# A two-layer recurrent trunk on one core: the adaLN modulation computed on VectorE, GpSimd and ScalarE instead of TensorE

## The chip, the core and the metric

One core of one Trainium2 chip runs the kernel. The metric is the device time of one execution in microseconds (us). TensorE (PE) multiplies matrices, VectorE (DVE), ScalarE (ACT) and GpSimd (POOL) do elementwise work, SyncE (SP) issues most DMAs. Each engine takes its own instructions in the order of the program; engines wait for one another by semaphores.

## What is computed

A decoder trunk of two layers over 1024 tokens of width 1024, all in float32. Layer 0 mixes tokens by RWKV-7, layer 1 by a gated DeltaNet; each is followed by a dense SwiGLU layer. Before each sublayer the tokens are scaled and shifted, and after it gated, by a modulation that depends on one vector `c` alone:

```python
cond = jax.nn.silu(c)                                   # c is (1, 1024)
for i in range(2):
    mod = (cond @ ada_w[i] + ada_b[i])[:, None, :]      # 1024 x 6144, every layer
    sh1, sc1, ga1, sh2, sc2, ga2 = jnp.split(mod, 6, axis=-1)
    u = x * (1 + sc1) + sh1
    y = mixer_i(u)                                      # RWKV-7, then gated DeltaNet
    x = layer_norm(ALPHA * x + (1 + ga1) * y)
    u = x * (1 + sc2) + sh2
    gate, up = jnp.split(u @ ffn_w_in[i], 2, axis=-1)
    x = layer_norm(ALPHA * x + (1 + ga2) * ((silu(gate) * up) @ ffn_w_out[i]))
```

RWKV-7 first interpolates each token with the one before it, in six mixtures (`lerp`): `k`, `v` and `r` are products of three of them with 1024x1024 weights, and three small ones (decay, rate, gate) of the others with 1024x64 or 1024x128 weights. The modulation is a matrix-vector product: 2 x 1024 x 6144 weights, 50 MB, each used once.

## The kernel before

**Tiles.** Features lie on the partitions in KT = 8 blocks of 128, tokens on the free axis, in two halves of 512. A large product is taken in float32 accuracy by three matmuls per block of 128x128: weight and operand are each split into a rounded part and a remainder (`split`, L220: ACT casts the rounded part, POOL or DVE subtracts it), and `mm3` (L261 to L266) adds hi x hi, hi x lo and lo x hi. One product of 128 rows with a half is 8 x 3 = 24 matmuls of 512 columns. `weight` (L241) loads 512 KB (tile `wr`, two buffers) and splits it into `wh` and `wl` (three buffers each); at the first use it also saves `wl` to DRAM, and at the second it loads it back, so that only ACT's cast (L252) is left.

**Stages**, with their places in the profiled execution. A (0 to 230 us): layer 0's modulation and the first half's k, v and r products. B (to 684): RWKV units of the first half, woven with the second half's products. C (684 to 1335): RWKV units of the second half, woven with dense work of the first (output projection, norm, SwiGLU layer) and with layer 1's modulation. Then a "turn" (1335 to some 1680): the second half's output projection, norms, and first products of the DeltaNet, among them those with the weights `w_g`. Then DeltaNet units woven with the second half's dense layer, a second turn, and the same for the other half.

`weave`, `interleave` and `drive` set the order in which pieces of two or three generators are recorded, by costs given by hand. A scheduler then places the instructions on each engine, so that the order on an engine is not simply that of the code.

**Modulation before** (`ada`, L279). The column of silu(c) lies in `condr`, 128 x 8 x 32, with zeros in 31 of 32 columns (`cond_columns`, L274). A matmul takes it as the stationary operand and 128 rows by 512 or 256 columns of the weights as the moving one (L296), in plain float32, with four blocks of k side by side in the array (`tile_position`). The four partial rows are copied by ACT (L301), transposed by PE (L305) so that the result lies along partitions, summed by DVE (L307), and the bias is added. Layer 0 takes 12 pieces of 512 columns, layer 1 takes 24 of 256. Loads come from SP, two of 512 KB a piece in layer 1, four in layer 0.

**Start before** (`proj_rwkv`, L355). Pieces 0 and 2 of layer 0 (shift and scale of the feature blocks 0 to 3) come first; then four tiles of x are modulated on DVE (`make_x`, L366) and mixed (`lerp`, L380); the first half of k of the first NH = 5 products follows with half weights (`half_weight`, `half_product`); pieces 1 and 3 are run between these, and the second half of k comes when they are done. In the loop behind it, each step loads and splits its own weight and small weight, and multiplies. `rest()` (in `main`) puts the other eight pieces between the products.

**Where layer 1's modulation lay**: 24 pieces in stage C alone, with PSUM banks of their own kind and one buffer for loaded weights.

Of the kernel before, what the change touches and what calls it, by code (L numbers as in the profile page):

```python
# [27 lines left out]
        ("lng", 32), ("lnb", 32), ("adab", 96), ("conv", 96), ("ng", 1), ("c", 8), ("alog", 8), ("dtb", 8)]  # L28
# [29 lines left out]
def body(ctx, tc, A):  # L58
# [55 lines left out]
    def mm_ps():  # L114
        return bank("mm")
# [9 lines left out]

    def ad_ps():
        return bank("ad")
# [140 lines left out]
    cond = tl(cp, [P, KT], F32, "cond")  # L268
    sigmoid(cond[:, :], V("c", 0, 8))
    tt(dve, cond[:, :], cond[:, :], V("c", 0, 8), MUL)  # L270
# [3 lines left out]
    def cond_columns(pl):  # L274
        condr = pools["condr"] = tl(pl, [P, KT, 32], F32, "condr")
        dve.memset(condr[:, :, :], 0.0)
        dve.tensor_copy(out=condr[:, :, 0], in_=cond[:, :])

    def ada(ap, l, j, n=512, bufs=4, ps=None, bk=mm_ps):  # L279

        condr = pools["condr"]
        w = 1024 // n
        pst = None
        for q in range(KT // w):
            raw = tl(ap, [P, w, n], F32, "ada", bufs)
            (act if q % 2 == 0 and not ps and ADQ and j > 3 else sync).dma_start(
                out=raw[:, :, :],
                in_=A["ada_w"][l, P * w * q:P * w * (q + 1), n * j:n * j + n].rearrange("(k p) c -> p k c", p=P))
            if ps:
                yield 1.0  # L290
            if pst is None:
                pst = (ps or bk)()
            for k in range(w):
                kt = w * q + k
                g = kt % 4
                pe.matmul(pst[32 * g:32 * g + 32, 0:n], condr[:, kt, :], raw[:, k, :], start=(kt < 4), stop=(kt >= 4),  # L296
                          tile_position=(0, 32 * g))
        if ps:
            yield 0.4
        row = e_tile()  # L300
        act.copy(out=row[:, 0:n], in_=pst[:, 0:n])  # L301
        pc = (ps or bk)()
        m = n // P
        for i in range(m):
            pe.transpose(pc[:, P * i:P * i + P], row[:, P * i:P * i + P], C("ident"))  # L305
        o = mod[l][:, m * j:m * j + m]
# [7 lines left out]
        elif f % 3 == 2:  # L314
            ts2(dve, o1, o, 1.0, (0.5 if f == 5 else 1.0) / ALPHA, ADD, MUL)
# [39 lines left out]
    def proj_rwkv():  # L355
# [72 lines left out]
        for k in range(4):  # L428
            load_x(0, k)
# [1196 lines left out]
```

## Time and profile before

| | us |
|---|---|
| three runs | 3346.52, 3362.83, 3360.3 |
| their median | 3360.3 |
| the profiled execution | 3353.55 |
| its span (first to last instruction) | 3351.8 |
| mean granted TensorE clock in it | 0.976 |

A row of a timeline reads: start in us, duration in us, engine, line, operation, out<-in by the program's names, shape, count of instructions put together, and in brackets the idle time of the engine just before and what ended it. A row of a group has the count, then busy us and mean ns, then idle time before. Chain of waits: PE's three matmul lines hold 10% each of the chain that ended last, no other line more than 1%. The busy tenths of PE, POOL and DMA in 40 equal slices of 84 us:

```profile
PE   7989999998999999898999999999999999999997
...
POOL 3563232355454443455521000230244543520001
...
DMA  7773334253445444645754555566654546565553
```

The first slice holds the start, in which PE is at seven tenths. The zeros of POOL are the stages of the DeltaNet units.

### The profile page before, as it was taken

What the parts mean: (1) busy time and instruction counts of PE and PEld (TensorE: products, weight loads), DVE (VectorE), ACT (ScalarE), POOL (GpSimd) and SP (SyncE); (2) the same over time, 40 slices, a digit from 0 to 9 for tenths busy, and PEclk for the clock granted to TensorE, in tenths of its full rate; (3) what the DMA queues carried; (4) which work ended last, traced back from release to release, by engine and by line L of the source; (5) the groups of instructions that cost most, each with busy time, mean ns of one, the idle gap of its engine ahead of it and who ended that gap; (6) DMA issues with size and microseconds to landing.
All of it is one profiled execution on the core that took longest, in us unless ns stands there. A gap on an engine that the chain in (4) does not pass through costs nothing. (4 is left out here: it accounts for less than half of the span.)

```text
span 3351.8 us, 52009 instructions
## 1 busy us (share of the span) xinstructions
PE 3189.0 (95%) x19152; PEld 2459.8 (73%) x19152; DVE 2073.8 (62%) x4549; ACT 1409.7 (42%) x2735; POOL 1133.4 (34%) x1354
## 2 busy tenths in 40 slices
PE   7989999998999999898999999999999999999997
PEld 4667777776777767676877778777777777878886
DVE  5557888888666666586476555575477653563235
ACT  4665777644333332355432322365432322332222
POOL 3563232355454443455521000230244543520001
PEclk8999999998999999999999999999999999999998
DMA  7773334253445444645754555566654546565553
GB/s 262 271 244 103 113 105 132 96 183 113 163 168 170 162 154 148 215 170 189 248 192 165 185 172 174 195 200 226 219 173 144 175 167 216 176 213 181 197 183 130
DMA packets 240527, 594.13 MB, mean 177 GB/s; under 512 B 24720, under 2 KB 80656, under 8 KB 240272
## 3 DMA queue, kind: packets, MB, share of 16 engines
q1 hardware_dynamic: 240128, 590.74, 51.9%
q8 instruction: 150, 2.46, 0.3%
q14 instruction: 105, 0.86, 0.1%
q10 hardware_dynamic: 144, 0.07, 0.0%
HBM read 440.04 MB, written 150.67 MB: 176 GB/s over the span
## 5 line engine op out<-in xcount | busy, mean ns | idle before, releaser
L264 PE MATMUL mm<-s,wh 128*128 128x512 f32 x2608 | 1076.9, 413 | 12.2 <-DVE e L215 5.4
L265 PE MATMUL mm<-s,wh 128*128 128x512 f32 x2608 | 1051.6, 403 | 12.3 <-POOL s L212 7.9
L266 PE MATMUL mm<-s,wl 128*128 128x512 f32 x2608 | 1046.0, 401 | 0.0
L212 POOL TENSOR_TENSOR wl<-wr,wh 128x256 fp32r<-128x256 f32 (+1 forms) x828 | 653.8, 821 | 845.3 <-ACT wh L222 784.1
L264 PEld LDWEIGHTS mm<-s,wh 128*128 128x128 f32 x2608 | 495.0, 190 | 131.3 <-issue 25.1
L265 PEld LDWEIGHTS mm<-s,wh 128*128 128x128 f32 x2608 | 495.7, 190 | 105.4 <-POOL s L212 11.9
L266 PEld LDWEIGHTS mm<-s,wl 128*128 128x128 f32 x2608 | 495.4, 190 | 93.1 <-issue 0.4
L252 ACT CAST wh<-wr 128x1024 fp32r<-128x1024 f32 x199 | 206.8, 1049 | 496.0 <-PE mm L265 238.5
L222 ACT CAST wh<-wr 128x1024 fp32r<-128x1024 f32 (+1 forms) x254 | 228.7, 906 | 342.0 <-PE mm L265 181.2
L215 DVE SCALAR_TENSOR_TENSOR x<-mm,modp,x 128x512 f32<-128x512 f32 x272 | 202.0, 747 | 76.6 <-PE mm L266 74.7
L264 PE MATMUL mm<-ys,wh 128*128 128x512 f32 x544 | 219.3, 403 | 5.8 <-DVE x L215 5.8
L265 PE MATMUL mm<-ys,wh 128*128 128x512 f32 x544 | 217.5, 400 | 0.0
L266 PE MATMUL mm<-ys,wl 128*128 128x512 f32 x544 | 217.2, 399 | 0.0
L215 DVE SCALAR_TENSOR_TENSOR e<-e,vec,e 128x512 f32<-128x512 f32 x144 | 124.1, 865 | 97.2 <-ACT e L1306 94.6
L212 DVE TENSOR_TENSOR e<-mm,e 128x512 f32<-128x512 f32 x88 | 60.6, 689 | 167.3 <-PE mm L266 167.0
L215 DVE SCALAR_TENSOR_TENSOR e<-e,mm 128x512 f32<-128x512 f32 x88 | 60.2, 684 | 144.8 <-ACT e L679 144.5
L838 PEld LDWEIGHTS <-z 128*128 128x128 f16 x1600 | 84.0, 98 | 82.8 <-issue 47.7
L215 DVE SCALAR_TENSOR_TENSOR tx<-mm,modp,tx 128x512 f32<-128x512 f32 x112 | 83.1, 747 | 78.5 <-PE mm L266 78.2
L212 DVE TENSOR_TENSOR s<-e,s 128x512 fp32r<-128x512 f32 x106 | 85.8, 811 | 69.5 <-ACT s L222 69.2
L264 PEld LDWEIGHTS mm<-ys,wh 128*128 128x128 f32 x544 | 103.7, 191 | 32.6 <-DVE x L215 6.6
L266 PEld LDWEIGHTS mm<-ys,wl 128*128 128x128 f32 x544 | 103.7, 191 | 25.7
L212 POOL TENSOR_TENSOR acc<-tx,tx 128x512 f32<-128x512 f32 x1 | 1.3, 1300 | 357.1 <-DVE tx L215 357.1
(395 smaller groups left out, 5492.2 us busy)
## 6 DMA issues: line engine op xcount, KB each, us to landing
wr<-w_in SPq DMA_DIRECT2D x176, 512.0 KB, 4.5
ada<-ada_w SPq DMA_DIRECT2D x96, 512.0 KB, 5.0
loi<-wl SPq DMA_DIRECT2D x88, 512.0 KB, 2.9
wr<-w_ffo SPq DMA_DIRECT2D x88, 512.0 KB, 5.0
wl<-loi SPq DMA_DIRECT2D x88, 512.0 KB, 3.6
wr<-w_g SPq DMA_DIRECT2D x64, 512.0 KB, 4.8
lof<-wl SPq DMA_DIRECT2D x44, 512.0 KB, 2.9
wl<-lof SPq DMA_DIRECT2D x44, 512.0 KB, 3.5
```

Of the source, the lines that this page charges most:

```text
L212: eng.tensor_tensor(out=out, in0=a, in1=b, op=op)
L215: return dve.scalar_tensor_tensor(out=out, in0=a, scalar=s, in1=b, op0=op0, op1=op1)
L222: act.copy(out=hi, in_=src)
L252: act.copy(out=hi[:, :], in_=raw[:, :])
L264: pe.matmul(out, wh[:, off:off + P], ah, start=start, stop=False)
L265: pe.matmul(out, wh[:, off:off + P], al, start=False, stop=False)
L266: pe.matmul(out, wl[:, off:off + P], ah, start=False, stop=stop)
L838: pe.matmul(out, l, r, start=start, stop=stop)
```

## The change

The weights `ada_w` are transposed ahead of the launch, so that row o of a block holds all 1024 weights of output o; `c` is given as a row. The kernel spreads the row over 128 partitions, takes silu of it (`cond_row`), and a modulation value is then the sum of one row's products with it: one "dot" of 128x1024 gives 128 outputs, already along partitions. 48 dots make a layer. In layer 0 a dot is one instruction of DVE that multiplies and sums. In layer 1 it is four multiplications of 128x256 on POOL, in place, and one copy on ACT that sums. The condition row is saved to DRAM and loaded again for layer 1, in two pools.

```diff
+    def cond_row(pl, first=False):
+        cr = pools["crow"] = tl(pl, [P, D], F32, "crow")
+        if first:
+            sync.dma_start(out=cr[:, :], in_=A["c_row"].to_broadcast([P, D]))
+            th = tl(pl, [P, D], F32, "ada", AD)
+            act.activation(out=th[:, :], in_=cr[:, :], func=AF.Tanh, scale=0.5)
+            dve.tensor_scalar(out=th[:, :], in0=th[:, :], scalar1=0.5, scalar2=0.5, op0=MUL, op1=ADD)
+            tt(dve, cr[:, :], cr[:, :], th[:, :], MUL)
+        else:
+            sync.dma_start(out=cr[:, :], in_=crow_d[:, :].to_broadcast([P, D]))
+    def ada_load(pl, l, j, bufs):
+        raw = raw_ada[l, j] = tl(pl, [P, D], F32, "ada", bufs)
+        sync.dma_start(out=raw[:, :], in_=A["ada_w"][l, j])
+    def ada_dot(l, j):
+        raw = raw_ada.pop((l, j))
+        if l:
+            for o in range(0, D, 256):
+                tt(pool, raw[:, o:o + 256], raw[:, o:o + 256], pools["crow"][:, o:o + 256], MUL)
+            act.activation(out=raw[:, :], in_=raw[:, :], func=AF.Copy, accum_out=mod[l][:, j:j + 1])
+            return
+        dve.scalar_tensor_tensor(out=raw[:, :], in0=raw[:, :], scalar=1.0, in1=pools["crow"][:, :], op0=MUL, op1=MUL,
+                                 accum_out=mod[l][:, j:j + 1])
+    def ada(pl, l, js, bufs, depth, cost):
+        js = list(js)
+        for n in range(depth):
+            ada_load(pl, l, js[n], bufs)
+        yield cost
+        for n, j in enumerate(js):
+            ada_dot(l, j)
+            if l:
+                yield cost
+            if n + depth < len(js):
+                ada_load(pl, l, js[n + depth], bufs)
...
+        for k in range(AHEAD):
+            step_load(k)
+            if k == 0:
+                quarter_load(0)
+        step_scale(0)
+        for k in range(KT):
+            make_x(0, k)
+            if k % 2 == 0:
+                for p in range(NH):
+                    quarter_weight(p, k // 2)
+                if k < 6:
+                    quarter_load(k // 2 + 1)
+            step_load(k + AHEAD)
+            if k < KT - 1:
+                step_scale(k + 1)
             lerp(0, 1, k)
+            for p in range(NH if k < 6 else 0):
+                if k == 0:
+                    begun[p] = mm_ps()
+                product(p, k)
...
-            banks(mm=5, ad=2, rows=1)
+            banks(mm=7, rows=1)
...
-                    yield from ada_rest(ap, 0, range(4, 12), 2.5, bufs=AD, bk=ad_ps)
+                    yield from ada(ap, 0, range(16, 48), AD, 3, 0.6)
...
-                    weave(parts(proj, 3 * KT), 150, rest(), 20, -LS)
+                    weave(parts(proj, 3 * KT), 150, rest(), 25, -LS)
...
-            weave(seq(*steps[:SB]), 16 * UC * W[0], parts(proj, 3 * KT - PP), 112, LD[0])
+            first, dense = seq(*steps[:SB]), parts(proj, 3 * KT - PP)
+            next(first)
+            drive(itertools.islice(dense, 10))
+            weave(first, 16 * UC * W[0], dense, 105, LD[0])
...
-            weave(seq(*steps[SB + S2:]), 16 * UC * W[1], interleave([dense, ada_rest(ap, 1, range(24), 1.0, n=256, bufs=1, ps=row_ps)], [390, 24 * 3.4 * AF_]), 390 + 24 * 3.4, LD[1], BURST)
+            weave(seq(*steps[SB + S2:]), 16 * UC * W[1], interleave([dense, ada(ap, 1, range(24), 1, 1, 0.05)], [390, 2.5 * AF_]), 391, LD[1], BURST)
...
-            weave(heads(gp, cg, 0), 8 * 42 * W[2], seq(proj_gdn(0, (4,)), ffn(0, 1, FY=FY)), 430, LD[2], BURST)
+            dense = interleave([seq(proj_gdn(0, (4,)), ffn(0, 1, FY=FY)), ada(pools["g"], 1, range(24, 48), 1, 1, 0.05)], [430, 2.5 * AF_])
+            weave(heads(gp, cg, 0), 8 * 42 * W[2], dense, 431, LD[2], BURST)
```

Further edits in `proj_rwkv`: the first five products take quarter weights, one contraction block at a time, as soon as the block of x is mixed; the x of the first half is modulated by ACT instead of DVE; weights are loaded and split up to two groups ahead (`ahead`) and small weights loaded one group ahead (`small_load`); during the r products the gate's mixture and the next x are asked for one step earlier. `prep1` gives up its turn once more in each first unit. Layer 1's 48 dots are recorded half in stage C and half with the first DeltaNet units.

**What stands where: DVE at the start.** Before, behind the constants (`mod` and `modp` are the modulation, `ad` a PSUM bank, `x` and `l` a token block and its mixture):

```order
L307 TENSOR_REDUCE mod_15_97<-ad_341 128x4
L374 MEMSET x_484 128x1
L212 TENSOR_TENSOR mod_15_97<-mod_15_97,vec_67 128x4
L313 TENSOR_SCALAR modp_17_99<-mod_15_97 128x4
L218 TENSOR_SCALAR x_356<-x_356,modp_17_99,mod_15_97 128x512
L218 TENSOR_SCALAR x_358<-x_358,modp_17_99,mod_15_97 128x512
L375 COPY utail_267<-x_356 128x1
L218 TENSOR_SCALAR x_360<-x_360,modp_17_99,mod_15_97 128x512
L215 SCALAR_TENSOR_TENSOR l_395<-x_356,vec_67,l_395 128x512
L375 COPY utail_267<-x_358 128x1
L215 SCALAR_TENSOR_TENSOR l_405<-x_358,vec_67,l_405 128x512
```

Of the change, at the same place (`ada` is a loaded block of weights, `crow` the condition row, `sx` the remainder of a mixture):

```order
L277 TENSOR_SCALAR ada_289<-ada_289 128x1024
L209 TENSOR_TENSOR crow_287<-crow_287,ada_289 128x1024
L296 SCALAR_TENSOR_TENSOR ada_293,mod_14_93<-ada_293,crow_287 128x1024
L296 SCALAR_TENSOR_TENSOR ada_295,mod_14_93<-ada_295,crow_287 128x1024
L209 TENSOR_TENSOR mod_14_93<-mod_14_93,vec_67 128x2
L301 TENSOR_SCALAR modp_16_95<-mod_14_93 128x1
L385 COPY utail_264<-x_297 128x1
L384 MEMSET x_319 128x1
L296 SCALAR_TENSOR_TENSOR ada_309,mod_14_93<-ada_309,crow_287 128x1024
L212 SCALAR_TENSOR_TENSOR l_368<-x_297,vec_67,l_368 128x512
L296 SCALAR_TENSOR_TENSOR ada_311,mod_14_93<-ada_311,crow_287 128x1024
L209 TENSOR_TENSOR sx_372<-l_368,sx_371 128x512
```

Before, DVE sums two pieces and then does four blocks of x after each other; now two dots stand in front of each block's mixture, and DVE holds no modulation of x.

**POOL in the `w_g` products of the turn** (`wl` the remainder of a weight, `wr` the loaded and `wh` the rounded one). Before:

```order
L212 TENSOR_TENSOR wl_19166<-wr_19163,wh_19165 128x256 x4
L212 TENSOR_TENSOR wl_19215<-wr_19212,wh_19214 128x256 x4
L212 TENSOR_TENSOR wl_19290<-wr_19287,wh_19289 128x256 x4
L212 TENSOR_TENSOR wl_19380<-wr_19377,wh_19379 128x256 x4
L212 TENSOR_TENSOR wl_19468<-wr_19465,wh_19467 128x256 x4
L212 TENSOR_TENSOR wl_19549<-wr_19546,wh_19548 128x256 x4
L212 TENSOR_TENSOR wl_19638<-wr_19635,wh_19637 128x256 x4
```

Of the change, for the same weights:

```order
L209 TENSOR_TENSOR wl_18718<-wr_18715,wh_18717 128x256 x4
L209 TENSOR_TENSOR ada_22481<-ada_22481,crow_17083 128x256 x4
L209 TENSOR_TENSOR wl_18769<-wr_18766,wh_18768 128x256 x4
L209 TENSOR_TENSOR ada_22689<-ada_22689,crow_17083 128x256 x4
L209 TENSOR_TENSOR wl_18849<-wr_18846,wh_18848 128x256 x4
L209 TENSOR_TENSOR ada_22905<-ada_22905,crow_17083 128x256 x4
L209 TENSOR_TENSOR wl_18939<-wr_18936,wh_18938 128x256 x4
L209 TENSOR_TENSOR ada_23107<-ada_23107,crow_17083 128x256 x4
L209 TENSOR_TENSOR wl_19029<-wr_19026,wh_19028 128x256 x4
L209 TENSOR_TENSOR ada_23322<-ada_23322,crow_17083 128x256 x3
L209 TENSOR_TENSOR wl_19115<-wr_19112,wh_19114 128x256 x4
L209 TENSOR_TENSOR ada_23322<-ada_23322,crow_17083 128x256
```

Between two neighbouring splits there now stand the four multiplications of one dot, each on the one buffer that the load behind the dot before it has filled.

**ACT ahead of the turn's partial sums** (`wh` with a load `wr` are the out projection's weights, L249 after and L252 before; `e` and `lt` other outputs of ACT). Before:

```order
L252 CAST wh_17706<-wr_17704 128x1024
L574 ACTIVATE e_17518<-x_10266 128x512
L574 ACTIVATE e_17523<-x_10388 128x512
L252 CAST wh_17740<-wr_17738 128x1024
L252 CAST wh_17781<-wr_17779 128x1024
L607 ACTIVATE e_17686<-mm_17667 128x128
L252 CAST wh_17849<-wr_17847 128x1024
L252 CAST wh_17917<-wr_17915 128x1024
```

Of the change:

```order
L294 ACTIVATE ada_19527,mod_15_94<-ada_19527 128x1024
L627 ACTIVATE e_17073<-x_10233 128x512
L249 CAST wh_17292<-wr_17290 128x1024
L294 ACTIVATE ada_19765,mod_15_94<-ada_19765 128x1024
L249 CAST wh_17333<-wr_17331 128x1024
L660 ACTIVATE e_17238<-mm_17219 128x128
L294 ACTIVATE ada_20000,mod_15_94<-ada_20000 128x1024
L249 CAST wh_17401<-wr_17399 128x1024
L294 ACTIVATE ada_20160,mod_15_94<-ada_20160 128x1024
L249 CAST wh_17469<-wr_17467 128x1024
L615 ACTIVATE lt_17324<-mm_17322 128x512
L294 ACTIVATE ada_20364,mod_15_94<-ada_20364 128x1024
```

Five sums of dots (L294, with `mod` as second output) have come between the casts of the projection's weights; each waits for POOL's multiplications of its own block.

More of the change, by code (lines that the diff above doesn't have):

```diff
@@ L279, in ada @@
[L279 to L306, printed above, removed]
-        dve.tensor_reduce(out=o, in_=pc[:, 0:n].rearrange("p (i g r) -> p i g r", i=m, g=4)[:, :, :, 0],
-                          axis=mybir.AxisListType.X, op=ADD)
-        tt(dve, o, o, V("adab", 48 * l + m * j, m), ADD)
-        f = (m * j) // 8
-        o1 = mod1[l][:, m * j:m * j + m]
@@ L312, in ada, with ada_scale @@
+    def ada_scale(l, f, o, o1):
         if f % 3 == 1:
@@ L443, in proj_rwkv, with quarter_load, quarter_weight @@
-        ws0 = {p: half_weight(p, 1) for p in range(NH)}
+        ws0, raw_w = {}, {}
+        def quarter_load(q):
+            for p in range(NH):
+                raw_w[p] = e_tile()[:, 0:256]
+                sync.dma_start(out=raw_w[p], in_=A["w_rkv"][1, p][:, 256 * q:256 * q + 256])
+        def quarter_weight(p, q):
+            o = 256 * (q % 2)
+            if o == 0:
+                ws0[p, q // 2] = s_tile(), s_tile()
+            split(raw_w.pop(p), *(t[:, o:o + 256] for t in ws0[p, q // 2]))
@@ L444, in proj_rwkv @@
         loaded.append(other_constants())
-        for k in range(4, KT):
-            lerp(0, 1, k)
+        sync.dma_start(out=crow_d[:, :], in_=pools["crow"][0:1, :])
         for (h, i), (h2, i2) in zip(order, order[1:]):
@@ L449, in proj_rwkv, with ahead @@
             acc = row_ps()
+            nxt_w = {}
+            def ahead(h, i, p):
+                if p < KT and p not in begun and (i, p) not in nxt_w:
+                    nxt_w[i, p] = weight(A["w_rkv"][i, p], None, ("r", i, p) if i != 1 or p >= NH else None)
             for grp in GROUPS[h]:
                 ws = {}
+                if h == 0:
+                    for p in (grp[0], grp[0] + 1) if grp[0] not in begun else (NH, NH + 1) if grp[0] == 0 else ():
+                        ahead(h, i, p)
                 for n in SMALL[i]:
@@ L481, in proj_rwkv @@
                         mm3(acc[:, :], ws.get(n) or small_weight(h, n, p), 0, made[h, 3 + n, p], p == 0 and n != 1, p == KT - 1 and n != 0)
+                    if i == 0 and h == 0 and p < KT - 1:
+                        lerp(0, 5, p + 1)
+                        load_x(1, p + 1)
                     if i == 0:
```

107 lines of the change are left out of this document (50 added, 57 removed).

## The prediction

> **What bounds the kernel now.** I read the profiled execution first as a whole (busy time per engine), then in stretches, then the single rows at the places that the change touches. All sums are made against that execution: a span of 3351.8 us and 3353.55 us with what lies around it. The median of the three timed runs is 6.8 us above it, so nothing under about 7 us could be told from the scatter of those runs, and 0.5% (17 us) is about what a measurement of this kernel can tell from no change.
>
> ```profile
> span 3351.8 us, 52009 instructions
> PE 3189.0 (95%) x19152; PEld 2459.8 (73%) x19152; DVE 2073.8 (62%) x4549; ACT 1409.7 (42%) x2735; POOL 1133.4 (34%) x1354
> ```
>
> PE is busy 95%, so a microsecond of matmul removed is a microsecond gained, as long as nothing else becomes late there. Next, busy time per stretch; the columns are the stretch, its length, and busy us (and instructions) of PE, weight load, DVE, ACT and POOL, then the granted clock, DMA share and GB/s.
>
> ```profile
> 20.00:40.00 20.00, 16.51 (x60) 10.20 (x61) 10.82 (x21) 8.03 (x14) 10.09 (x10) 0.74 0.99 362
> 74.00:230.50 156.50, 148.75 (x724) 109.47 (x723) 85.10 (x133) 98.40 (x167) 81.15 (x103) 0.98 0.80 271
> 236.00:262.00 26.00, 17.52 (x97) 13.51 (x97) 11.80 (x20) 13.00 (x33) 18.43 (x27) 0.74 0.45 138
> 690.00:900.00 210.00, 197.07 (x1335) 144.44 (x1328) 158.85 (x421) 86.08 (x178) 105.56 (x128) 0.93 0.45 149
> 900.00:1335.00 435.00, 416.86 (x2846) 312.21 (x2846) 291.71 (x782) 149.98 (x322) 193.16 (x263) 0.99 0.47 157
> 1335.00:1620.00 285.00, 261.96 (x1218) 201.25 (x1217) 177.80 (x267) 133.84 (x217) 152.29 (x168) 0.95 0.57 199
> 1620.00:1680.00 60.00, 59.15 (x264) 48.51 (x263) 29.39 (x44) 29.28 (x56) 31.63 (x38) 1.00 0.75 258
> ```
>
> In every stretch PE is nearly full, with two exceptions: the start and 236 to 262 us. POOL, which receives the second layer's products, is half busy from 690 to 1680.
>
> **First layer.** Removed from PE: the modulation matmuls and their transposes, and with them the order of the start, in which four pieces of 512 modulation columns had to be summed before the last lerps. The PE timeline shows three marks of that start.
>
> ```profile
> 22.83 1.31 PE L264 MATMUL mm<-sx,s 128*128 128x512 f32 x2 [3.65 <-ACT sx L222]
> ...
> 53.36 0.79 PE L264 MATMUL mm<-sx,s 128*128 128x512 f32 x1 [4.57 <-ACT sx L222]
> ...
> 80.32 0.40 PE L264 MATMUL mm<-sx,wh 128*128 128x512 f32 x1
> 80.55 0.39 PE L265 MATMUL mm<-sx,wh 128*128 128x512 f32 x1
> ```
>
> The first product starts at 22.83, its second half of k at 53.36, and the sixth product (the first with a whole weight, `wh`) at 80.32. The last two rows stand 0.23 us apart: that is one steady matmul of 512 columns (0.2275 over longer rows). The projections of the stage end at about 230.5.
>
> Added to DVE: 48 dots of 128x1024. The profile has none; the nearest rows are two-input operations of 512 columns on DVE, and the same kinds as groups of the stretch 74 to 231, with POOL's subtractions.
>
> ```profile
> 24.73 1.15 DVE L212 TENSOR_TENSOR sx<-l,sx 128x512 fp32r<-128x512 f32 x1
> ```
>
> ```profile
> 68.02 0.69 DVE L212 TENSOR_TENSOR s<-l,s 128x512 fp32r<-128x512 f32 x1
> ```
>
> ```profile
> L215 DVE SCALAR_TENSOR_TENSOR l<-x,vec,l 128x512 f32<-128x512 f32 x43 | 36.2, 859 | 16.8 <-ACT l L389 16.3
> ```
>
> ```profile
> L212 POOL TENSOR_TENSOR wl<-wr,wh 128x256 fp32r<-128x256 f32 x78 | 66.5, 883 | 68.4 <-ACT wh L222 46.6 <-DMA wr<-w_l 13.1 <-DMA lor<-wl 8.7
> ```
>
> Undisturbed, 512 columns take 0.69 us; beside POOL's splits 1.15. A dot is twice as wide, so I estimate 1.2 us alone (bounds 0.7, no dearer than one of 512 columns, and 2.3, always disturbed). The start then goes in k-steps of two dots (2.4), a lerp of two operations (1.3), small operations (0.4) and POOL's disturbance (0.5 to 1): 4.6 to 5.1 us. The condition row and two loads come first, so the first product starts at about 15, and the eighth step is done at about 15 + 8 x 4.9 = 54.
>
> From 54 on PE still has 19 products of 24 matmuls and 72 small ones, 528 x 0.2275 = 120 us, plus some 5 us of the last two k-steps and sums: it could end at 180 (**-50**). DVE has the own work of the stretch, 85.1 us, disturbed. At 0.69 instead of a mean 0.859 that is 68, less some 2 us of modulation adds: 66. The 32 remaining dots add 38. Disturbance: before, DVE lost 85.1 - 66 = 19 us to 81.15 us of POOL, of which the share 85.1/156.5, 44 us, fell beside it: 0.44 per us. Now DVE is nearly always busy, so 81 x 0.44 = 36. 54 + 66 + 38 + 36 = 194; with the 8 us for which PE waited in that stretch before (156.5 - 148.75) and the last product after the last operand (27 x 0.2275 = 6) I get 208, and take 210: **-20**. The DMA row below is a bound that is not reached: 62.39 MB at the 362 GB/s of the second window above is 172 us.
>
> ```profile
> DMA packets 30273, 62.39 MB, mean 270 GB/s; under 512 B 2720, under 2 KB 6240, under 8 KB 30258
> ```
>
> The Trainium skill, page "SBUF — State Buffer", section "Who interferes with whom", says that a VectorE instruction with two SBUF inputs contends with a GpSimd instruction that reads SBUF, for a shared pair of ports locked exclusively. By it each us of POOL would stop DVE for as long, against the 0.44 above; the rows 1.15 and 0.69 agree with contention, but no row shows a complete stop.
>
> The new split of weights two groups ahead and the small weights loaded early are priced at nothing: ACT (98.40 of 156.5) and POOL (81.15) have room, and PE hardly waited there. If the cover is gone, the loss is inside the 8 us already counted.
>
> **Start of stage B.** Two waits of PE, at low clock, stand here:
>
> ```profile
> 242.13 0.58 PE L264 MATMUL p<-l2h,l2h 128*128 128x256 f32 x1 [6.29 <-ACT l2h L222]
> ```
>
> ```profile
> 251.83 0.70 PE L1065 MATMUL p<-t,cst 128*128 128x256 f32 x2 [1.89 <-DVE t L1062]
> ```
>
> The change issues ten pieces of projections (30 matmuls, 6.8 us) ahead of the first unit. They can fill both waits (8.2 us): **-8**, bounds 0 and -10.
>
> **Second layer, gain.** PE loses 48 groups of modulation matmuls and 24 pairs of transposes. What such a group takes on PE is read from the start of the next instruction.
>
> ```profile
> 1012.68 0.64 PE L296 MATMUL rows<-ada,condr 128*32 128x256 f32 x8
> 1013.25 0.50 PE L264 MATMUL mm<-s,wh 128*128 128x512 f32 x1
> ...
> 1023.54 0.38 PE L305 MATMUL rows<-cst,e 128*128 128x128 f32 x2
> 1023.85 1.71 PE L1075 MATMUL p<-ar,bk 64*128 64x128 f32 x16
> ```
>
> 0.57 and 0.31 us: 48 x 0.57 + 24 x 0.31 = 34.8 us, from 689.8 to 1326.7 as the tile's row says.
>
> ```profile
> L296 PE MATMUL rows<-ada,condr x384: 379/403/636, 689.8 to 1326.7; 128*32 128x256 f32 x192
> ```
>
> **Second layer, cost.** Each dot is now a closed loop, since there is one buffer: load (issued by SP, which waits for the sum before), four multiplies on POOL, one sum on ACT. All three engines take their instructions in order, and the new order puts 24 dots into the first third of stage C and 24 around the turn, with other work between: splits of weights, partial sums, the units' operations. If a turn of the loop is longer than what PE has to do between two such neighbours, PE waits. Rows for one turn:
>
> ```profile
> ada<-ada_w SPq DMA_DIRECT2D x16, 512.0 KB, 3.8
> ```
>
> ```profile
> wr<-w_g SPq DMA_DIRECT2D x26, 512.0 KB, 4.3
> ```
>
> ```profile
> 695.47 2.80 POOL L212 TENSOR_TENSOR wl<-wr,wh 128x256 fp32r<-128x256 f32 x4 [4.33 <-DMA ada<-ada_w]
> ...
> 899.57 3.27 POOL L212 TENSOR_TENSOR wl<-wr,wh 128x256 fp32r<-128x256 f32 x4
> ...
> 1600.66 3.73 POOL L212 TENSOR_TENSOR wl<-wr,wh 128x256 fp32r<-128x256 f32 x4 [1.17 <-ACT wh L222]
> ...
> 1655.06 3.72 POOL L212 TENSOR_TENSOR wl<-wr,wh 128x256 fp32r<-128x256 f32 x4 [1.57 <-ACT wh L222]
> ```
>
> ```profile
> L252 ACT CAST wh<-wr 128x1024 fp32r<-128x1024 f32 x199 | 206.8, 1049 | 496.0 <-PE mm L265 238.5
> ```
>
> Landing 3.8 (690 to 900) or 4.3 (the turn's weights), four multiplies 2.8 to 3.7, a pass of ACT over 1024 columns 1.05, and 0.5 to 1.2 for handovers and what stands ahead in a queue: 8.2 to 10.3. I take 9.0 in C and 9.2 in the turn. Nothing excludes 11, where DMA, POOL and ACT each meet other work.
>
> In C, 24 turns of 9.0 are 216 us from 691: 907. The work behind the last of them started at 899.57 before (the second row), so the loop is +8, +10 for turns that stand behind longer pieces on POOL, -5.5 for the one weight (24 x 0.2275) that PE holds already split: **+12**. Of the 34.8 us of PE, 16 of 48 loads fell before 900, where the loop sets the pace and nothing is gained; 2/3 remain: **-23**.
>
> In the turn four dots stand in a row before the first partial sum, one between each two casts of out-projection weights on ACT. There PE needs 5.46 us a weight: 4 x (9.2 - 5.5) = +15. Seven dots alternate one to one with the splits of `w_g`; before, ten such splits took 1655.06 - 1600.66 = 54.4 us, 5.44 each: 7 x (9.2 - 5.44) = +26. Less two weights already split (11) and 4.1 us that PE waited for POOL's splits there anyway:
>
> ```profile
> PE mm L265 <- POOL s L212: 4.1, 3, 2.7
> ```
>
> **+26**. The sum: -20 - 8 + 12 - 23 + 26 = -13, so 3353.55 - 13 = about **3341 us**.
>
> **Rivals.**
> 1. The loop stays hidden (turns near 8 us, and weights far enough ahead). For it: POOL and ACT are half idle in every stretch from 690 to 1680. Against it: PE at 99% in 1620 to 1680, with splits at its own pace. -20 - 8 - 35, and 5 given back: -58, **3296**.
> 2. Slower: the closed loop is the bound, at the same two places, with turns of 11 us. Each us per turn costs 24 in C and 11 in the turn, 35 us. Break-even is at 9.2 + 13/35 = 9.6, slower by 0.5% from 10.0, and at 11 it is 3341 + 63 = **3404**. For it: the four POOL rows grow to 3.73 in the turn; DMA is at 0.75 there. Against: landing is 3.8 in C.
> 3. The first layer gains nothing, since VectorE and GpSimd exclude each other. POOL's 81 us of the stretch at their undisturbed 0.73 per 0.883 are 67, all added to DVE: 54 + 66 + 38 + 67 = 225, +2 for the end: -3 instead of -20, **3358**. The skill's rule named above is this one.
> 4. The first layer becomes PE-bound, at -50: the dots at 0.7, or DVE's work not needed so early: **3311**.
>
> **How the numbers follow.** Forecast 0.35 (its own range 3326 to 3356), rival 1 0.22, rival 2 0.20, rival 3 0.13, rival 4 0.10. Faster by over 0.5% (under 3337): rivals 1 and 4 whole, 0.32, and 0.14 of the forecast's 0.35: 0.46. Slower (over 3370): 0.18 of rival 2, 0.03 of rival 3, 0.02 of the forecast: 0.23. Within 0.5%: 0.31. The range reaches to rival 1 below and to a loop turn of 10.6 us above (3341 + 35 x 1.4 = 3390): 3294 to 3390.
>
> **What would show it.** Right: the sixth product begins near 55 and stage A ends near 210 with DVE nearly full and dots of 1.2 us; loads of `ada` follow each other by 9 us in C; PE's new waits are for POOL's splits or ACT's casts in the turn. Wrong: PE as full as before from 1335 to 1620 (rival 1); distances between loads over 10 us (rival 2); DVE full and stage A no shorter (rival 3); PE full after 55 (rival 4). The forecast falls most easily with the length of one loop turn, which is put together from rows of other work.

## The result and the profile after

| | us |
|---|---|
| before, four runs | 3346.52 to 3362.83, median 3355.99 |
| the change, four runs | 3428.39 to 3430.77, median 3429.55 |
| ratio | 1.0224, 95% interval 1.0202 to 1.0245 |
| span of the profiled execution | 3351.8 before, 3426.8 after |

The change is slower by 2.2%, 74 us; the forecast was 13 us faster, and the time lies beyond the range given. Of all runs below, one (of the four of e4) took 11826.78 us and is left out. The page of the changed kernel, its first line and the busy time of the engines:

```profile
span 3426.8 us, 51063 instructions
...
PE 3155.0 (92%) x18480; PEld 2466.3 (72%) x18480; DVE 2138.7 (62%) x4570; ACT 1451.3 (42%) x2813; POOL 1295.3 (38%) x1546
```

PE is busy 34 us less and nevertheless idle 109 us longer (3426.8 - 3155.0 = 272, against 163). More than 34 us of work was taken from it: without the modulation's matmuls and transposes, the other 18480 matmuls cover 3119.7 us in the trace before, 69 less than all. The same 18480 cover 3155.0 us after, 35 us more, at a mean granted clock of 0.962 against 0.976. POOL has 162 us more. Where the time went is read from the same instruction in both traces: how much later it starts after the change.

| instruction | before, us | after | later by | added since the mark above | the sum's term |
|---|---|---|---|---|---|
| ScalarE's copy of the last of the 24 first-half products (end of stage A) | 234.9 | 238.1 | 3 | 3 | -20 |
| first unit's first matmul of `ar` and `bk` | 252.5 | 267.8 | 15 | 12 | -8 |
| the 293rd of the 512 such matmuls (start of C) | 678 | 692 | 14 | -1 | 0 |
| the 366th of them (19 of the 24 loads for dots in C are out) | 849 | 895 | 46 | 32 | |
| first load of the turn (`yr`) | 1338 | 1363 | 26 | -20 | (both C rows) -11 |
| first matmul of a DeltaNet unit (end of the turn) | 1685 | 1759 | 75 | 49 | +26 |
| first store of the second half's result | 3344 | 3419 | 75 | 0 | 0 |

Each of the four came out worse. Busy time by stretches of the changed kernel, at the stretches that answer to those before (columns as there):

```profile
232.00:262.00 30.00, 20.71 (x86) 15.25 (x84) 15.73 (x18) 16.99 (x36) 20.54 (x30) 0.83 0.58 181
262.00:690.00 428.00, 406.15 (x3878) 315.24 (x3878) 358.93 (x997) 296.73 (x789) 127.40 (x176) 0.99 0.34 111
690.00:950.00 260.00, 211.87 (x1291) 160.71 (x1291) 175.46 (x425) 115.03 (x235) 187.76 (x235) 0.86 0.44 146
950.00:1357.00 407.00, 388.96 (x2550) 304.50 (x2550) 284.76 (x740) 145.99 (x306) 197.89 (x264) 0.98 0.38 129
1357.00:1700.00 343.00, 285.42 (x1267) 216.93 (x1265) 184.16 (x271) 158.45 (x266) 229.12 (x262) 0.91 0.59 203
```

Where the dots of the second layer stand (690 to 950 and 1357 to 1700), PE falls to 81% and 83% of the stretch, and the granted clock to 0.86 and 0.91. POOL is at 72% and 67%, against 50% and 53% before. The new groups, with what ended the idle time before them:

```profile
L209 POOL TENSOR_TENSOR ada<-ada,crow 128x256 f32<-128x256 f32 x192 | 154.1, 830 | 66.3 <-DMA ada<-ada_w 59.0 <-ACT x L690 4.9 <-ACT e L682 2.2
```

```profile
L294 ACT ACTIVATE ada<-ada 128x1024 f32<-128x1024 f32 x48 | 50.8, 1058 | 193.3 <-POOL ada L209 193.3
```

```profile
L296 DVE SCALAR_TENSOR_TENSOR ada<-ada,crow 128x1024 f32<-128x1024 f32 x48 | 66.3, 1385 | 13.6 <-DMA ada<-ada_w 13.5
```

ACT stood idle 193 us in front of the 48 sums: 4.0 us each, with all of its other work behind. One such place, on POOL and then on ACT (start, duration, and in brackets the idle time before):

```profile
741.83 1.29 POOL L209 TENSOR_TENSOR acc<-x,x 128x512 f32<-128x512 f32 x1
743.07 3.01 POOL L209 TENSOR_TENSOR ada<-ada,crow 128x256 f32<-128x256 f32 x3
746.05 1.73 POOL L209 TENSOR_TENSOR acc<-acc,x 128x512 f32<-128x512 f32 x1
747.74 1.74 POOL L209 TENSOR_TENSOR e<-e,e 128x512 f32<-128x512 f32 x1
749.44 1.41 POOL L209 TENSOR_TENSOR nl<-sa,nh 64x256 f16<-64x256 f32 x2
750.92 1.28 POOL L209 TENSOR_TENSOR acc<-acc,x 128x512 f32<-128x512 f32 x1
752.16 1.16 POOL L209 TENSOR_TENSOR nd<-nh,diag 128x512 f16<-128x512 f16 x1
753.28 0.74 POOL L209 TENSOR_TENSOR ada<-ada,crow 128x256 f32<-128x256 f32 x1
```

```profile
754.05 1.06 ACT L294 ACTIVATE ada<-ada 128x1024 f32<-128x1024 f32 x1 [7.89 <-POOL ada L209]
755.01 0.19 ACT L294 ACTIVATION_READ_ACCUMULATOR ada<-ada 128x1 f32 x1
755.11 1.03 ACT L219 CAST wh<-wr 128x1024 fp32r<-128x1024 f32 x1
```

POOL works without a gap; the fourth multiplication of the dot waits 7 us behind partial sums and the units' `nl` and `nd`, which themselves stood behind the first three. ACT waits 7.89 us for it, and a weight's cast stands behind the sum. This is a chain of queues, not one slow operation.

### The profile page after: what moved, and what is told of

Same layout as the page of the kernel before. It is cut to its first block, busy times and chain, and to the rows that moved or that the text cites. A ratio compares the mean times of both kernels' runs of the same rounds, so it can differ in the third digit from the quotient of the medians.

```text
span 3426.8 us, 51063 instructions
## 1 busy us (share of the span) xinstructions
PE 3155.0 (92%) x18480; PEld 2466.3 (72%) x18480; DVE 2138.7 (62%) x4570; ACT 1451.3 (42%) x2813; POOL 1295.3 (38%) x1546
## 5 line engine op out<-in xcount | busy, mean ns | idle before, releaser
L263 PE MATMUL mm<-s,wl 128*128 128x512 f32 x2608 | 1060.0, 407 | 2.6 <-POOL wl L209 2.1
L209 POOL TENSOR_TENSOR wl<-wr,wh 128x256 fp32r<-128x256 f32 (+1 forms) x828 | 669.1, 839 | 765.5 <-ACT wh L219 722.8
L261 PEld LDWEIGHTS mm<-s,wh 128*128 128x128 f32 x2608 | 500.9, 192 | 142.7 <-ACT wh L219 22.7
L262 PEld LDWEIGHTS mm<-s,wh 128*128 128x128 f32 x2608 | 502.1, 193 | 118.7 <-POOL s L209 22.1
L263 PEld LDWEIGHTS mm<-s,wl 128*128 128x128 f32 x2608 | 502.3, 193 | 102.8 <-POOL wl L209 6.6
L249 ACT CAST wh<-wr 128x1024 fp32r<-128x1024 f32 x199 | 206.5, 1048 | 481.7 <-PE mm L262 210.6
L209 POOL TENSOR_TENSOR ada<-ada,crow 128x256 f32<-128x256 f32 x192 | 154.1, 830 | 66.3 <-DMA ada<-ada_w 59.0
L294 ACT ACTIVATE ada<-ada 128x1024 f32<-128x1024 f32 x48 | 50.8, 1058 | 193.3 <-POOL ada L209 193.3
```

The costliest lines, as they stand in the source:

```text
L209: eng.tensor_tensor(out=out, in0=a, in1=b, op=op)
L249: act.copy(out=hi[:, :], in_=raw[:, :])
L261: pe.matmul(out, wh[:, off:off + P], ah, start=start, stop=False)
L262: pe.matmul(out, wh[:, off:off + P], al, start=False, stop=False)
L263: pe.matmul(out, wl[:, off:off + P], ah, start=False, stop=stop)
L294: act.activation(out=raw[:, :], in_=raw[:, :], func=AF.Copy, accum_out=mod[l][:, j:j + 1])
```

## Experiments

Sixteen kernels ran; the table has those that bear on the second layer. Its columns say how much later than before (us) the instructions of the table above start; "last store" is the first store of the second half's result. The last column but one, the last store less the start of C, holds what stage C, the turn and what follows cost, that is the second layer's part, free of what the first layer's part did ahead of it. These columns come from one profiled execution each: e6 and e9, for instance, lost 5 to 10 us more than the change near 310 us, in stage B, where their edits change nothing. Each ratio is taken against the kernel before on the same chip.

| kernel | first unit | start of C | in C (849) | end of turn (1685) | last store | C and turn | ratio (95%) |
|---|---|---|---|---|---|---|---|
| the change | +15 | +14 | +46 | +75 | +75 | +61 | 1.0224 (1.0202 to 1.0245) |
| e1 first layer's part alone | +15 | +15 | +14 | +18 | +22 | +7 | 1.0048 (1.0030 to 1.0067) |
| e2 second layer's part alone | +15 | +10 | +51 | +77 | +83 | +73 | 1.0222 (1.0194 to 1.0251) |
| e3 loads pinned | +14 | +14 | +44 | +76 | +89 | +75 | 1.0260 (1.0228 to 1.0292) |
| e5 no sums | +14 | +13 | +50 | +40 | +41 | +28 | 1.0152 (1.0125 to 1.0179) |
| e6 no multiplications | +18 | +25 | +28 | -8 | -9 | -34 | 0.9965 (0.9950 to 0.9981) |
| e7 load, multiplications, sum pinned | +15 | +15 | +32 | +36 | +39 | +24 | 1.0118 (1.0101 to 1.0135) |
| e9 dots on VectorE | +15 | +22 | +33 | +7 | +10 | -12 | 1.0009 (0.9993 to 1.0026) |
| e11 half the multiplications | +14 | +14 | +33 | +27 | +27 | +13 | 1.0075 (1.0038 to 1.0112) |
| e12 before, with dots on VectorE | -1 | 0 | +7 | -18 | -20 | -20 | 0.9932 (0.9905 to 0.9958) |

**Which layer.** e1 takes the second layer's part back: `cond_columns`, the old `ada` with its matmuls and `ada_rest` are put in again for layer 1, and the two weaves are as before.

```diff
-            weave(seq(*steps[SB + S2:]), 16 * UC * W[1], interleave([dense, ada(ap, 1, range(24), 1, 1, 0.05)], [390, 2.5 * AF_]), 391, LD[1], BURST)
+            weave(seq(*steps[SB + S2:]), 16 * UC * W[1], interleave([dense, ada_rest(ap, 1, range(24), 1.0, n=256, bufs=1, ps=row_ps)], [390, 24 * 3.4 * AF_]), 390 + 24 * 3.4, LD[1], BURST)
...
-            dense = interleave([seq(proj_gdn(0, (4,)), ffn(0, 1, FY=FY)), ada(pools["g"], 1, range(24, 48), 1, 1, 0.05)], [430, 2.5 * AF_])
-            weave(heads(gp, cg, 0), 8 * 42 * W[2], dense, 431, LD[2], BURST)
+            weave(heads(gp, cg, 0), 8 * 42 * W[2], seq(proj_gdn(0, (4,)), ffn(0, 1, FY=FY)), 430, LD[2], BURST)
```

> The first layer, its start, the weights ahead and the start of stage B as after the change; the second layer's modulation on TensorE as before. Theory A (the stage table of the two traces: the first layer's part costs +13 us by 680 us, the second layer's +62): about 3368 us, some 13 us above before, and 60 below the change. Rival B (the parts work on each other: a second layer on PE fills waits that the first layer's part leaves): within 5 us of before. Rival C (most of the loss is the first layer's, only showing late): over 3390 us.

Measured: 3374.9 us, before on the same chip 3357.5, so +17. e2 is the reverse: the kernel before, with `cond_row`, `ada_dot` and `ada` (here `ada_row`) of the change for layer 1.

```diff
+                    cond_row(ap, True)
+                    sync.dma_start(out=crow_d[:, :], in_=pools["crow"][0:1])
...
-            cond_columns(ap)
+            cond_row(ap)
...
-            weave(seq(*steps[SB + S2:]), 16 * UC * W[1], interleave([dense, ada_rest(ap, 1, range(24), 1.0, n=256, bufs=1, ps=row_ps)], [390, 24 * 3.4 * AF_]), 390 + 24 * 3.4, LD[1], BURST)
+            weave(seq(*steps[SB + S2:]), 16 * UC * W[1], interleave([dense, ada_row(ap, 1, range(24), 1, 1, 0.05)], [390, 2.5 * AF_]), 391, LD[1], BURST)
```

> The first layer, start and stage B as before; the second layer's modulation on GpSimd and ScalarE as after the change. The condition row is made once more in the first stage, on ScalarE and VectorE. Theory A: +12 us in stage C and +50 in the turn, so about 3418 us. Rival B: under 3390 us. Rival C: within 15 us of before.

Measured: 3432.1 us, +75, of which 12 came in stage A, where the row is made besides (the copy of the 24th product at 246.7 instead of 234.9 us). Some three quarters of the loss is the second layer's; the first layer's part is a loss too, not the gain of 28 us that I had put down. Theory A holds in direction for both.

**Is it the closed loop?** e3 queues each load behind the weight load before it:

```diff
-        sync.dma_start(out=raw[:, :], in_=src)
+        last_w[0] = sync.dma_start(out=raw[:, :], in_=src)
...
-        sync.dma_start(out=raw[:, :], in_=A["ada_w"][l, j])
+        with tc.issue_after(last_w[0].ins) if l else ExitStack():
+            sync.dma_start(out=raw[:, :], in_=A["ada_w"][l, j])
```

> The change, with each load of a second layer's dot queued on SP behind the weight load that stands before it in the program, so that 24 dots spread over stage C and 24 over the DeltaNet units. Theory A (a closed loop of 10.7 us a turn, packed into 254 us of stage C and 314 us around the turn, paces PE there): the losses at 700 to 950 and 1360 to 1700 go, PE keeps its 35 us; about 3345 to 3365 us. Rival B (GpSimd's 154 us of multiplications delay the splits of weights wherever they stand): over 3400 us.

Measured: 3444.0 us, slower still. The dots did spread (from 695 to 1309 and from 1603 to 2149 us), the loss did not go. In C nothing was gained after 900 either, and 33 us were lost from the first dot behind C (1603 us) to the end of the turn, over seven dots. So a loss of this size needs no closely packed loop. Alone the run does not rule the loop out as the cause in the change, because the pinned loads made POOL wait as well: 232 us of idle time in front of the multiplications until their load had landed, against 59 in the change. e9 below says more. ACT's idle time in front of the sums was 206.6 us, more than in the change:

```profile
L297 ACT ACTIVATE ada<-ada 128x1024 f32<-128x1024 f32 x48 | 50.8, 1059 | 206.6 <-POOL ada L209 206.6
```

**Which engine.** e5 leaves the sums out, e6 the multiplications, e11 two of the four.

```diff
-            act.activation(out=raw[:, :], in_=raw[:, :], func=AF.Copy, accum_out=mod[l][:, j:j + 1])
```

> The change without the 48 sums on ScalarE (the second layer's modulation stays zero, set once by VectorE); loads and GpSimd's multiplications remain. Theory A (the sum stands on ScalarE's queue ahead of casts and copies that PE needs, and waits there for load and multiplications: 193 us of idle time of ScalarE in the change): nearly all of the second layer's 62 us go, 3345 to 3375 us. Rival B (GpSimd's multiplications delay the splits of weights): over 3405 us.

```diff
-            for o in range(0, D, 256):
-                tt(pool, raw[:, o:o + 256], raw[:, o:o + 256], pools["crow"][:, o:o + 256], MUL)
```

> The change without GpSimd's 192 multiplications (the sums take the loaded weights alone). Theory A: ScalarE still waits for each load, some 3.5 us a turn instead of 3.5 plus 2.8 to 3.7, so about half of the 62 us remains: 3385 to 3410 us. Rival B: the 62 us go, 3335 to 3370 us.

```diff
-            for o in range(0, D, 256):
+            for o in range(0, D // 2, 256):
```

> The change with two of GpSimd's four multiplications of each second layer's dot (half of each sum is left without its factor). Theory A (the cost grows with GpSimd's busy time, 154 us for 89 us of loss): half of the loss comes back, 3375 to 3395 us. Rival B (the cost is one of waits, per dot, whatever the multiplications take): over 3405 us.

Measured: 3401.6, 3341.0 and 3380.5 us: e5 lies between its two theories, e6 is its rival B, e11 its theory A. In C and the turn: +28 without sums, -34 without multiplications, +13 with half of them, against +61. Without multiplications the whole of PE's 34.8 us is there. The multiplications cost 61 + 34 = 95 us for 154 us of POOL's time, 0.6 us for each us, and half of them half as much (48). That speaks for a cost that grows with POOL's time, not for one of waits per dot: POOL's own waits for these loads were no shorter with half of them (72.9 us, against 59.0). The sums cost 33 us, and only because the multiplications are there: in e6 ACT still did all 48.

e7 records load, multiplications and sum in three places and ties each to its own engine's last load, split or cast:

```diff
+            with tc.issue_after(last_split[0].ins):
+                for o in range(0, D, 256):
+                    tt(pool, raw[:, o:o + 256], raw[:, o:o + 256], pools["crow"][:, o:o + 256], MUL)
...
                 yield cost
+                with tc.issue_after(last_cast[0].ins):
+                    act.activation(out=raw[:, :], in_=raw[:, :], func=AF.Copy, accum_out=mod[l][:, j:j + 1])
```

> The change with load, multiplications and sum of each second layer's dot recorded in three separate places of the program and each queued behind the weight load, split or cast recorded before it, so that none stands first in its queue while the one before it is under way. Theory A: ScalarE no longer waits, 3340 to 3370 us. Rival B: over 3400 us, since GpSimd still does all multiplications.

Measured: 3390.6 us, between the two theories. ACT's wait fell from 193 to 44 us, and 37 us of the loss went with it, about what e5 gives (33):

```profile
L323 ACT ACTIVATE ada<-ada 128x1024 f32<-128x1024 f32 x48 | 50.7, 1056 | 43.9 <-POOL ada L209 43.9
```

What remains, 58 us above e6, comes with the multiplications on POOL. How much of it is their own time and how much is POOL's waiting for their loads, 213 us here, was not taken apart. e9 gives the second layer's dots to VectorE, as in the first:

```diff
     def ada_dot(l, j):
         raw = raw_ada.pop((l, j))
-        if l:
-            for o in range(0, D, 256):
-                tt(pool, raw[:, o:o + 256], raw[:, o:o + 256], pools["crow"][:, o:o + 256], MUL)
-            act.activation(out=raw[:, :], in_=raw[:, :], func=AF.Copy, accum_out=mod[l][:, j:j + 1])
-            return
```

> The change with the second layer's dots on VectorE, one instruction each as in the first layer; GpSimd and ScalarE have no part in them. Theory A (what costs is GpSimd's queue: the run without multiplications was 89 us below the change): most of that comes back, less up to 24 x 1.22 = 29 us in stage C, where VectorE is in the units' chain: 3345 to 3380 us. Rival B (any engine with the dots in its queue makes the units late by the same wait for loads): over 3400 us.

Measured: 3357.7 us, no difference from before. In C and the turn -12, so 22 of PE's 35 us are lost to 48 dots on VectorE and their loads, against 95 on POOL and ACT. It also speaks against the loop's pace as the cause: from load to load a turn takes 12.1 us in C (703.94 to 982.64), longer than the change's 10.7, and yet C loses 11 us from its start to the mark at 849, where the change loses 32. e12 takes the first layer from before, and 16 of these dots into C and 32, with two buffers, to the DeltaNet units:

```diff
+            cond_row(ap)
             dense = seq(out_proj(0, 0), norm0(0, 0), ffn(0, 0, FY=FY))
+            weave(seq(*steps[SB + S2:]), 16 * UC * W[1], interleave([dense, ada_row(ap, 1, range(16), 1, 1, 0.05)], [390, 2.5 * AF_]), 391, LD[1], BURST)
...
+            dense = interleave([seq(proj_gdn(0, (4,)), ffn(0, 1, FY=FY)), ada_row(pools["g"], 1, range(16, 48), 2, 2, 0.05)], [430, 2.5 * AF_])
```

> The kernel before, with its first layer untouched and the second layer's modulation as dots on VectorE: 16 in stage C, 32 with the DeltaNet units; the condition row is made twice from c. Theory A: PE's 35 us are gained and VectorE loses at most 16 x 1.22 = 20 us of it in stage C: 3320 to 3345 us, faster than both kernels. Rival B: within 10 us of before, or slower.

Measured: 3334.3 us against 3354.5, ratio 0.9932 (0.9905 to 0.9958): 20 us faster than before, as theory A had it, and faster than the change.

**The first layer.** e8 leaves out the 32 dots behind the start and their loads, e10 the dots alone, e16 the dots and three quarters of each load's bytes.

```diff
-                    yield from ada(ap, 0, range(16, 48), AD, 3, 0.6)
+                    dve.memset(mod1[0][:, 16:48], 1.0)
```

> The change without the first layer's 32 dots between the first projections and without their loads (the gate of the first sublayer is left at one and the modulation of the second at zero and one). Theory A (dots and their loads make VectorE late, as my sum for stage A had it): the stage's last projections end by 205 instead of 232 us, and the time is 20 us or more below the change. Rival B (PE waits for a weight's cast on ScalarE, which stands behind the copy of the product before; no dot is in that chain): the stage ends at 222 or later.

```diff
-                    yield from ada(ap, 0, range(16, 48), AD, 3, 0.6)
+                    dve.memset(mod1[0][:, 16:48], 1.0)
+                    yield from ada_loads(ap, 0, range(16, 48), AD, 3, 0.6)
...
+    def ada_loads(pl, l, js, bufs, depth, cost):
...
+            raw_ada.pop((l, j))
+            if n + depth < len(js):
+                ada_load(pl, l, js[n + depth], bufs)
```

> As the run without dots behind the start, but the 32 loads of the first layer's weights stay, only the dots on VectorE are left out (the gate of the first sublayer is one, the modulation of the second zero and one). Theory A (VectorE's time in the stage: 32 dots of 1.2 us): stage A ends at about 187 us as in the run without both. Rival B (the loads, on SP's queue and the DMA engines, make the weights late): it ends at 215 or later.

```diff
-        sync.dma_start(out=raw[:, :], in_=A["ada_w"][l, j])
+        n = 256 if l == 0 and j >= 16 else D
+        sync.dma_start(out=raw[:, 0:n], in_=A["ada_w"][l, j, :, 0:n])
```

> As the run with the 32 loads but without their dots, each load now of 256 columns (128 KB) instead of 1024; the same parts of the modulation are left out. Theory A (bytes: the stage moves some 62 MB at some 270 GB/s and is bound by that): the 24th product is copied at 195 to 210 us, near the run without loads (199.6). Rival B (places on SP's queue): at 222 us or later, near the run with full loads (227.3).

Measured, as the copy of the 24th product: 238.1 in the change, 199.6 in e8, 227.3 in e10, 199.0 in e16 (times 3386.8, 3421.8 and 3383.1 us). So e8 and e16 follow their theory A, e10 its rival B. The dots themselves are worth 11 us of the stage, the loads 28, and it is their bytes rather than their places in the queue: with as many loads of a quarter of the size the stage is as short as with none. The same 126 us in the kernel before, the change, e8, e10 and e16, in this order (the last two numbers are the DMA share and GB/s):

```profile
74.00:200.00 126.00, 118.52 (x582) 86.08 (x581) 68.64 (x105) 80.50 (x138) 69.48 (x87) 0.97 0.79 267
```

```profile
74.00:200.00 126.00, 101.31 (x398) 75.96 (x396) 101.84 (x149) 73.66 (x128) 68.48 (x74) 0.92 0.76 265
```

```profile
74.00:200.00 126.00, 120.68 (x530) 95.32 (x529) 95.78 (x117) 91.59 (x158) 87.23 (x99) 1.00 0.64 213
```

```profile
74.00:200.00 126.00, 101.86 (x410) 77.12 (x409) 67.36 (x93) 72.58 (x125) 64.88 (x79) 0.93 0.78 270
```

```profile
74.00:200.00 126.00, 121.99 (x548) 97.80 (x547) 94.18 (x119) 92.51 (x164) 90.41 (x99) 1.00 0.74 244
```

Wherever all bytes are loaded, 265 to 270 GB/s pass, whatever PE and VectorE do; what PE was spared it then waited. It waited for casts of weights (from 0 to 232 us; us in total, times, longest):

```profile
PE mm L261 <- ACT wh L219: 26.7, 12, 5.7
```

In the order of the changed kernel most such casts stand behind the copy of the product before it, where before they stood one or two products ahead. e13 turns that by an edge, e14 takes the edit out that should split weights ahead.

```diff
+                    with tc.issue_after(last_cast[0].ins) if h == 0 and last_cast[0] is not None else ExitStack():
+                        act.copy(out=o[:, :], in_=pst[j][:, :])
```

> The change, with the copy of each first-half product on ScalarE queued behind the cast of the weight recorded last before it, so that the next product's cast stands ahead of it. Theory A (PE waits 27 us in the first stage for casts that stand behind the copy of the product before): stage A ends at 205 to 222 us instead of 232, and the time is 10 to 25 us below the change. Rival B (the weights land late because of the loads on SP, so the cast waits for its load instead): stage A ends at 228 or later, time within 6 us of the change.

```diff
-                    for p in (grp[0], grp[0] + 1) if grp[0] not in begun else (NH, NH + 1) if grp[0] == 0 else ():
-                        ahead(h, i, p)
```

> The change without the loading and splitting of weights up to two groups ahead. Theory A (in the order the casts have no lead with the edit or without it, so it brings nothing): within 6 us of the change. Rival B (the edit is what hides the splits, as I had priced it at nothing with them hidden): 10 us or more above the change. Rival C (it takes the lead away): 10 us or more below.

Measured: 3425.4 us (ratio 1.0206, 1.0191 to 1.0221) with the 24th copy at 233.6, and 3432.8 us (1.0233, 1.0216 to 1.0250) at 241.0. Neither interval is clear of the change's (1.0202 to 1.0245), so e13 is its rival B and e14 its theory A. The place of the cast is not the main cause: with it turned, the copy came 4.5 us earlier in the one trace, and PE still waited 25.7 us for casts up to 232 us, against 26.7. And splitting weights ahead changes nothing that can be measured here. One thing stays open: in e8 and e16, casts stand one to three products ahead as well, so bytes and order changed together there; e13 has the order with all bytes, at one product ahead, and gained little.

e4 takes back the ten pieces ahead of the first unit:

```diff
-            first, dense = seq(*steps[:SB]), parts(proj, 3 * KT - PP)
-            next(first)
-            drive(itertools.islice(dense, 10))
-            weave(first, 16 * UC * W[0], dense, 105, LD[0])
+            weave(seq(*steps[:SB]), 16 * UC * W[0], parts(proj, 3 * KT - PP), 112, LD[0])
```

> The change, with the start of stage B as before (no ten pieces ahead of the first unit, weave at 112). Theory A (stage B is bound by its units, so ten pieces ahead of the first unit, +12 us, come out late at the end of it): 8 to 12 us less than the change, about 3419 us. Rival B (the ten pieces fill waits and the loss of the stage has another cause): 0 to 8 us more than the change.

Measured: 3423.7 us (1.0204, 1.0168 to 1.0239); first unit +8 instead of +15, start of C +6 instead of +14. In the trace 7 to 8 us, near theory A's 8 to 12; in the times not separable from the change, so neither theory is confirmed. e15 puts e9, e13 and e4 together, each with the edit shown there:

```diff
-        if l:
...
+                    with tc.issue_after(last_cast[0].ins) if h == 0 and last_cast[0] is not None else ExitStack():
...
+            weave(seq(*steps[:SB]), 16 * UC * W[0], parts(proj, 3 * KT - PP), 112, LD[0])
```

> The change with the second layer's dots on VectorE, the copy behind the next weight's cast in the first stage, and the start of stage B as before. Theory A: 3358 us of the run with dots on VectorE, less 10 to 25 for the casts and some 5 for the start of B: 3325 to 3345 us. Rival B: within 6 us of the run with dots on VectorE alone.

Measured: 3337.1 us against 3355.8, ratio 0.9952 (0.9934 to 0.9969): 19 us faster than before, where e9 was even with it. In the traces the first unit starts 5 us earlier than in the change with the edge alone (e13, 262.8 us), 7 with the start alone (e4, 260.9) and 13 with both (255.0), so each seems to give its share, though neither alone can be told in the times. The rest of the difference to e9 lies behind the first unit and was not tried apart.

## Why the prediction was wrong, step by step

**Second layer's gain, 34.8 us: right.** e6 has -34 in the column of C and the turn.

**Second layer's cost, +12 in C and +26 in the turn: the step that failed most.** I priced a closed loop by its turn (9.0 and 9.2 us) and let it act only where it is slower than what stands beside it. Measured, 24 turns took 695.26 to 949.05 us in C, 10.6 each, and those in the turn 13.1 (1386.26 to 1700.05). At my own 24 us per us of turn, 1.6 us more is 38 in C; C lost 32 up to the mark at 849 us and 38 by 989 us, behind the last dot, and got back 27 by the turn, where I had put 23. With both measured turns rival 2's prices even give 3341 + 24 x 1.6 + 11 x 3.9 = 3422 us. So rival 2 named the places and nearly the size. But that nearness is luck, since its mechanism, the loop as bound, does not hold: in e9 a turn in C is longer and costs a third, and in e7 turns of 27 us in C and 23 behind it cost less than half (+24 against +61). What failed is that the sum has no term for what 154 us of multiplications on POOL delay outside their own loop: POOL was taken as half idle and so as free. Half idle by busy time, it had the units' and the splits' operations spread over all of it, and every us of multiplications cost 0.6 us (e6, e11); that it does so through the units' and the weights' operations behind them is read from the order at 741 to 755 us, not tried by itself. ACT's half idle time was broken up by waits at the head of its queue (e5, e7).

**First layer, -20: failed at what bounds the stage.** I took VectorE to set its length, and wrote that the bound of 62.39 MB at 362 GB/s, 172 us, is not reached. VectorE was busy 131.84 of the 177 us from 55 to 232 (74%); without its 32 dots the stage ended 11 us earlier (e10), and with a quarter of their bytes another 28 (e16). 362 GB/s was the rate of 20 us. Over the stage 270 GB/s had passed before (62.39 MB up to 231 us), and 263 after (60.83 MB): the change took PE's work out of the stage, not the bytes, and the length went with the bytes. Before, PE's 95% in it hid that. The start itself went as told (first product at 17.58 us where I had 15, the sixth at 61.40 where I had 55 and before had 80.32, its weight loaded 27 us earlier), and 12 us of it were left at the fifth product's copy (68.6 instead of 80.5); the rest of the stage gave them back.

**The dots, 1.2 us: right** (1.208 at least, 1.385 on average). Rival 3, exclusion of VectorE and GpSimd, had nearly the right time for the stage, but not for its reason: without the 32 dots it was still 227.3 us long (e10). That the two hold each other up does show. A dot with no POOL instruction beside it, and one beside four of POOL's subtractions, which took 4.59 us beside this and other two-input operations of VectorE (2.80 was the least above):

```profile
101.93 1.22 DVE L296 SCALAR_TENSOR_TENSOR ada<-ada,crow 128x1024 f32<-128x1024 f32 x1
```

```profile
113.13 1.75 DVE L296 SCALAR_TENSOR_TENSOR ada<-ada,crow 128x1024 f32<-128x1024 f32 x1
```

```profile
111.48 4.59 POOL L209 TENSOR_TENSOR wl<-wr,wh 128x256 fp32r<-128x256 f32 x4
```

Of the 48 dots, 24 had nothing of POOL beside them and took 1.22 us on average; 12 had POOL busy for their whole length and took 1.67. In 11 of these 12, the dot and the POOL instructions beside it took together at least their undisturbed times added up. That agrees with the rule of the Trainium skill, page "SBUF — State Buffer", section "Who interferes with whom", by which the shared pair of ports is an exclusive lock. What rival 3 had wrong is the price: it added all of POOL's 67 us to VectorE, and half of the dots met no POOL instruction at all.

**Weights ahead, priced at nothing: right in size** (e14), though not by the cover I named: the order gives most casts no lead at all.

**Start of B, -8: wrong sign.** The wait was not filled, it has another releaser:

```profile
242.89 0.80 PE L261 MATMUL mm<-s,wh 128*128 128x512 f32 x1 [7.22 <-ACT wh L219]
```

The ten pieces wait there for a weight's cast of their own, and the first unit stands behind them.

## What to carry to other kernels

Before work is moved to an engine that is half idle, look at what else stands in that engine's queue and who waits for it: here 154 us on POOL cost 95, and the same dots on VectorE, as single instructions, 22. Before a stage is called bound by PE at 95%, look at its bytes too, and take the rate that the whole stage shows, not that of the best 20 us; whether bytes or work set its length, a run with fewer bytes and the same number of loads can tell. A waiting instruction in front of others costs by what stands behind it: three engines in a row for one dot, each in order, is three such places.

## What the hardware showed that I had not expected

Idle gaps of PE were followed by a lower granted clock, so a gap costs more than its length. The clock records of the two traces know only the whole clock and half of it. It stood at half for 160 us before and for 264 after. In the 3.4 us ahead of a drop (behind 300 us) PE was idle 60% of the time before and 67% after, on average, where it was idle 3% and 5.5% of the whole. The mean over stage C is 0.97 before and 0.93 after, and 0.86 in the stretch with the dots, where it was 0.94 before.

And the DMA share stayed at 0.76 to 0.79 in the first stage with PE waiting for weights; what keeps it from the 0.99 of 20 to 40 us was not tried. One candidate is on record: from 70 to 235 us SP's queue, which issues the loads, stood 45 us in front of stores that waited for ACT's copies of products and 46 in front of stores that waited for POOL's remainders (30 and 39 before, 18 and 40 in e16), with loads behind them.
